# Merge of a hybrid attention block: three shared staging places for both branches' outputs, and w_out loaded block by block

## The chip, the cores and the metric

One core of a Trainium2 chip runs the whole kernel. The metric is the device time of one execution in microseconds (us), as the median of several. Five engines work side by side, each on its own list of instructions in a fixed order: PE multiplies matrices, DVE (vector), ACT (scalar) and POOL (GpSimd) work on tiles, and SP (sync) issues most of the DMA transfers. An instruction that waits holds back everything behind it on its own engine.

## The reference, cut to what matters

```
proj = rms_norm(x) @ w_in              # split into q, k, v, gates of two branches
o_diff = differential attention (4 heads), normalised, times silu(gate)   # (1024, 512)
o_mla  = latent attention (4 heads), times silu(gate)                     # (1024, 512)
merged = sigmoid(g_diff) * (o_diff @ w_proj_diff) + sigmoid(g_mla) * (o_mla @ w_proj_mla)
x = x + merged @ w_out                 # w_out is 1024 x 1024
return rms_norm(x, norm_final)
```

All is float32. Each factor of a product is split into a high part (`...h`, a cast on ACT) and a low part (`...l`, the rest, a subtraction on DVE or POOL), and a product of tiles is three PE instructions: high by high, low by high, high by low (`mm3`, L160 to L162). The product with w_out is a scheme of seven products of half-size blocks, for which sums and differences of blocks of w_out are made first.

## The kernel before, in words

The differential branch runs first; its outputs are written to DRAM (`d_od`, four heads of 128 x 1024). The latent branch follows and writes its outputs to `d_om`. Gates are kept in DRAM as `d_t`. The merge begins while the last latent head is still in work:

- `merge_begin` makes the pools and loads the differential outputs: 8 half tiles of 128x512 (256 KB each) from `d_od` into the tile `or`, of which there is one, and splits each into `odh` (ACT) and `odl` (DVE). A load into a tile starts only when the last reader of the earlier content is done.
- Then `product(0, j)` multiplies them by w_proj_diff, for eight column blocks j in the order `JO`, in two halves of 12 PE instructions each. For each half a gate tile `tg` (three places) is loaded, and DVE multiplies it with the product in PSUM: the eviction, L1023, into `part` or `mr`. There are two PSUM banks `mm` for all this, so a half can start when the eviction of an earlier one has freed a bank. The weights come by `load_p` through `wpr`, are cast to `wph` on ACT and get `wpl` from POOL.
- The first two blocks j of `product(0, ...)` are mixed with the last values step of the latent branch (`mla_values`: transposes L457, split into `ph` and `pl`, products into `pv`). `take` loads the latent outputs from `d_om` through `omr` (two places) in the meantime and splits them into `omh`, `oml`.
- The remaining six blocks, `JO[2:]`, follow. Meanwhile w_out (4 MB) comes in three bursts: `load_b1` (four loads of 256 KB), `load_b2` (four of 512 KB), `load_b12` (four of 256 KB), and `weight_sums(i)` splits the blocks and makes their sums on DVE and POOL (L1128, L1138).
- Then `product(1, j)` for all eight j (latent outputs, no change), and the products with w_out.

When each piece of work is put into the program is set by `defer(ns, fn)`: it is called when a count of nominal PE time has moved on by ns. The order on each engine is settled when the program is built.

Of the kernel before, what the change touches and what calls it, by code (L numbers as in the profile page):

```python
# [14 lines left out]
F32 = mybir.dt.float32  # L15
# [8 lines left out]
P = 128  # L24
# [27 lines left out]
def emit(tc, a):  # L52
    nc = tc.nc
    V, A, G, T = nc.vector, nc.scalar, nc.gpsimd, nc.tensor

    def pool(name, side=None, space=None, bufs=1):
        kw = {}
        if side:
            kw["side"] = side
        if space is not None:  # L60
            kw["space"] = space
        return tc.alloc_tile_pool(name=name, bufs=bufs, reuse_waits="tile", **kw) if space is not DRAM \
            else tc.alloc_tile_pool(name=name, bufs=bufs, **kw)
# [3 lines left out]
    def nm(s):  # L67
        counter[0] += 1
        return f"{s}_{counter[0]}"

    def mk(p, shape, dt, tag, bufs=None):
        return p.tile(shape, dt, name=nm(tag), tag=tag, bufs=bufs)

    def one(p, shape, dt, name):
        return p.tile(shape, dt, name=name, tag=name, bufs=1)
# [14 lines left out]
    def defer(ns, fn):  # L90
        counter[0] += 1
        heapq.heappush(later, (clock[0] + ns, counter[0], fn))
# [18 lines left out]
    def drain():  # L111
        while queue or hook:
            fill(1.0)
# [5 lines left out]
    def drive(gen):  # L119
        for gap in gen:  # L120
            fill(gap)
# [29 lines left out]
    def split(hi, lo, src, eng=None):  # L151
        A.copy(hi, src)  # L152
        (eng or V).tensor_tensor(lo, src, f32(hi), op=ALU.subtract)  # L153
# [10 lines left out]
    def half(n):  # L164
        return slice(n * 512, n * 512 + 512)
# [191 lines left out]
    for si, (base, width, nw) in enumerate(sweeps):  # L357
# [28 lines left out]
        for b in range(NB):  # L386
            raw = mk((p0b, p0c)[si], [P, 384], F32, "raw", 8)
# [452 lines left out]
    def latent_tiles(h):  # L840
        pl = (latent["even"], pl2)[h % 2]
        kns[h] = [mk(pl, [P, S], F32R, "kn" + x, 1) for x in "hl"]
        qns[h] = [mk(pl, [P, S], F32R, "qn" + x, 1) for x in "hl"]
# [8 lines left out]
    def prep(h):  # L852
        w = latent_w.pop(h)
        if h % 2 == 0:
            st = [mk(pl2, [P, S], F32R, f"mqs{m}", 1) for m in range(2)]
            qrs[h], qrs[h + 1] = st
            yield from up(w[2], [0, 1, 2],
                          lambda b, n: qr_use(h, b, n, st))
        if h:
            yield from up_q(h, w)  # L860
        if h < 3:
            latent_w[h + 1] = load_latent_w(h + 1)
# [51 lines left out]
    def mla_group_scores(h, g):  # L914
        pend = None
        for i in range(4 * g, 4 * g + 4):
            cost, normalise = mla_scores(h, i)
            if pend:
                pend()
            pend = normalise  # L920
            yield cost
        pend()
        yield 0

    def mla_values(h, g, gap):
        u = mk(wk, [P, 512], F32, "u", 2)
        nc.sync.dma_start(u, d_mg[h][:, half(g)])
        probs = [mprobs.pop((h, i)) for i in range(4 * g, 4 * g + 4)]
        ov = yield from values(g, probs, lambda kb: mvf[g][:, blk(h)] if kb == 4 * g + 3 else
                                 (mvh[kb][:, blk(h)], mvl[kb][:, blk(h)]), tp_any, gap)  # L930
        o = mk(wk, [P, 512], F32, "g", 2)
        V.tensor_tensor(o, ov, u, op=ALU.mult)
        if (h, g) != (3, 1):
            nc.sync.dma_start(d_om[h][:, half(g)], o)
        else:
            split(p3["o"][1][0][3][:, half(1)], p3["o"][1][1][3][:, half(1)], o)
# [30 lines left out]
    def merge_begin():  # L967
        pb = p3["b"] = pool("p3b", "right")
        p3["o"] = [[], []], [[], []]
        p3["o"][1][0].extend(one(pb, [P, S], F32R, f"omh{k}") for k in range(4))  # L970
        p3["o"][1][1].extend(one(pb, [P, S], F32R, f"oml{k}") for k in range(4))
        for tag, shape, dt, bufs in (("wpr", [P, 4, P], F32, 2), ("wph", [P, 4, P], F32R, 2),
                                     ("wpl", [P, 4, P], F32R, 2), ("tg", [P, 512], F32, 3),
                                     ("omr", [P, 512], F32, 2), ("part", [P, 512], F32, 4)):
            for _ in range(bufs):
                mk(pb, shape, dt, tag, bufs)
        pa = p3["a"] = pool("p3a", "right")
        for k in range(4):
            h_ = one(pa, [P, S], F32R, f"odh{k}")
            l_ = one(pa, [P, S], F32R, f"odl{k}")  # L980
            for n in range(2):
                r = mk(pa, [P, 512], F32, "or", 1)
                nc.sync.dma_start(r, d_od[k][:, half(n)])
                split(h_[:, half(n)], l_[:, half(n)], r)
            p3["o"][0][0].append(h_)
            p3["o"][0][1].append(l_)
        p3["w"] = deque()
        p3["plan"] = deque((br, j) for br in range(2) for j in JO)
        for _ in range(2):
            load_p()  # L990

    def load_p():
        if p3["plan"]:
            br, j = p3["plan"].popleft()
            pa = p3["b"]
            wr = mk(pa, [P, 4, P], F32, "wpr", 2)
            nc.sync.dma_start(wr, a[("w_pd", "w_pm")[br]][j])
            wh = mk(pa, [P, 4, P], F32R, "wph", 2)
            wl = mk(pa, [P, 4, P], F32R, "wpl", 2)
            split(wh, wl, wr, G)  # L1000
            p3["w"].append((wh, wl))
# [32 lines left out]
    def group_and_next(h):  # L1034

        other = up_k(h + 1, latent_w[h + 1])
        for i, cost in enumerate(mla_group_scores(h, 1)):
            yield cost
            if i < 2:
                for _ in range(2):  # L1040
                    yield next(other)

    for h in range(4):
        if h < 3:
            latent_tiles(h + 1)
            queue.append(group_and_next(h))
        else:
            queue.append(mla_group_scores(h, 1))
        drive(mla_values(h, 0, 1300))
        drain()  # L1050
        if h < 3:
            queue.append(prep(h + 1))
            drain()
            if h == 2:
                p2v.release()
                latent["even"].release()
                latent["w"].release()
                latent["pool"].release()
                merge_begin()
            queue.append(mla_group_scores(h + 1, 0))  # L1060
        else:
            pl2.release()
            pb = p3["b"]
            queue.append(product(0, JO[0], done_d))
            queue.append(product(0, JO[1], done_d))

            def take(k, n):
                r = mk(pb, [P, 512], F32, "omr", 2)
                nc.sync.dma_start(r, d_om[k][:, half(n)])
                defer(3500, lambda: split(p3["o"][1][0][k][:, half(n)], p3["o"][1][1][k][:, half(n)], r))  # L1070

            for n in range(2):
                for k in range(4 - n):
                    defer(1500 * (4 * n + k), lambda k=k, n=n: take(k, n))
            fill(4000)
        drive(mla_values(h, 1, 700))
        drain()
# [17 lines left out]
    b11 = [one(p3w, [P, 512], F32, f"b11_{i}") for i in range(4)]  # L1095
    b12 = [one(p3w, [P, 512], F32, f"b12_{i}") for i in range(4)]
    b2 = [one(p3w, [P, D], F32, f"b2_{i}") for i in range(4)]

    def load_b1():
        for i in range(4):  # L1100
            nc.sync.dma_start(b11[i], a["w_out"][i][:, half(0)])

    def load_b2():
        for i in range(4):
            nc.sync.dma_start(b2[i], a["w_out"][4 + i])

    def load_b12():
        for i in range(4):
            nc.sync.dma_start(b12[i], a["w_out"][i][:, half(1)])

    def left_operand(n, i, src):
        t = left_set[n, i] = mk(p3["s"], [P, 2, 512], F32R, f"a{n % 2}{i}", 1)
# [2 lines left out]
    def right_operand(n, i, src, eng=None):  # L1115
        t = right_set[n, i] = mk(p3["d"] if n % 3 == 2 else p3w, [P, 2, 512], F32R, f"b{n % 3}{i}", 1)
        split(t[:, 0], t[:, 1], src, eng)
# [12 lines left out]
    def weight_sums(i):  # L1130

        b21, b22 = b2[i][:, half(0)], b2[i][:, half(1)]
        right_operand(0, i, b11[i])
        right_operand(1, i, b21)
        sub(G, b11[i], b12[i], b11[i])
        sub(V, b12[i], b22, b12[i])
        sub(V, b21, b21, b22)
        G.tensor_tensor(b21, b21, b11[i], op=ALU.add)  # L1138

    defer(1000, load_b1)  # L1140
    defer(6000, load_b2)
    defer(11000, load_b12)
    for i in range(4):
        defer(18000 + 5000 * i, lambda i=i: weight_sums(i))
    for j in JO[2:]:
        queue.append(product(0, j, done_d))
    drain()
# [198 lines left out]
```

## Time and profile before

| | |
|---|---|
| median of 3 runs | 909.52 us (907.31 to 910.62) |
| the profiled execution | 907.61 us, of which its trace spans 905.9 us |
| PE busy | 870.4 us (96%) |
| DVE, ACT, POOL busy | 580.5, 349.1, 286.9 us |
| mean granted clock of PE | 0.984 of full speed |

Times in the rows further down count from the start of the span. The merge's differential products lie between 700.8 and 774.2 us of it.

### The profile page before, as it was taken

The page shows a single profiled execution, that of the slowest core. Times are in us where ns is not written, and L with a number is a line of the kernel's source. Part 1 is how long each engine was busy: PE and PEld are TensorE (multiplying, and loading weights), DVE is VectorE, ACT ScalarE, POOL GpSimd, SP SyncE. Part 2 cuts the span into 40 slices and gives each one's busy share as a digit, 9 for nine tenths or more (in the row PEclk, how much of TensorE's full clock was granted, in tenths as well). Part 3 has the DMA queues.
Part 4 walks back from the last instruction along what each step waited for, and adds up shares of the span by engine and source line. Part 5 has one row for each costly group of instructions (what it writes and reads, how often), then busy time and mean ns, then how long its engine had stood idle before and what let it go on. Part 6 is the DMA issues. An engine that isn't in the chain of part 4 may idle for free.

```text
span 905.9 us, 11737 instructions
## 1 busy us (share of the span) xinstructions
PE 870.4 (96%) x4308; PEld 709.7 (78%) x4308; DVE 580.5 (64%) x1064; ACT 349.1 (39%) x690; POOL 286.9 (32%) x207
## 2 busy tenths in 40 slices
PE   9989999999999999999999999999999788999995
PEld 6879988787887878878777877688787476888884
DVE  5573257738287573874768485866867474689765
ACT  6652162334224242133423344545546340113442
POOL 2432013222241131422213222732313026485651
PEclk9999999999999999999999999999999797999998
DMA  8874035121222322312211216301025373435004
GB/s 291 292 204 137 22 128 175 59 82 70 82 71 69 93 71 71 93 50 90 94 33 58 76 56 221 99 13 47 24 62 183 127 264 107 140 117 209 1 24 164
DMA packets 49979, 96.74 MB, mean 107 GB/s; under 512 B 5120, under 2 KB 17664, under 8 KB 49920
## 3 DMA queue, kind: packets, MB, share of 16 engines
q1 hardware_dynamic: 47328, 89.81, 30.2%
q0 software_dynamic: 1152, 3.67, 1.3%
q10 hardware_dynamic: 1440, 2.49, 0.7%
q8 instruction: 34, 0.56, 0.3%
q14 instruction: 25, 0.20, 0.1%
HBM read 68.96 MB, written 27.00 MB: 106 GB/s over the span
## 4 chain that ended last, share of the span: by engine, by line
PE 80%; DVE 7%; DMA 6%; ACT 2%; issue 2%; POOL 2%; SPq 0%; POOLq 0%; DVEq 0%; ACTq 0%
PE mm L160 18%; PE mm L162 17%; PE mm L161 17%; PE sc L619 4%; PE acc L160 2%; PE acc L162 2%; PE acc L161 2%; PE tp L457 2%; PE bank L161 2%; PE bank L160 2%; PE bank L162 2%; PE pv L161 2%; PE pv L160 2%; PE pv L162 2%; DMA big<-in_xT 1%
## 5 line engine op out<-in xcount | busy, mean ns | idle before, releaser
L160 PE MATMUL mm<-hh,wh 128*128 128x512 f32 x512 | 205.9, 402 | 0.0
L162 PE MATMUL mm<-hh,wl 128*128 128x512 f32 x512 | 200.2, 391 | 0.0
L161 PE MATMUL mm<-hl,wh 128*128 128x512 f32 x512 | 199.9, 390 | 0.0
L153 POOL TENSOR_TENSOR wl<-wr,wh 128x1024 fp32r<-128x1024 f32 x32 | 81.8, 2557 | 240.2 <-ACT wh L152 240.2
L160 PEld LDWEIGHTS mm<-hh,wh 128*128 128x128 f32 x512 | 96.2, 188 | 25.0 <-issue 3.8
L162 PEld LDWEIGHTS mm<-hh,wl 128*128 128x128 f32 x512 | 96.1, 188 | 21.1
L161 PEld LDWEIGHTS mm<-hl,wh 128*128 128x128 f32 x512 | 96.3, 188 | 18.0
L438 ACT ACTIVATE e<-sc,mn 128x128 f32<-128x128 f32 (+3 forms) x64 | 47.5, 743 | 82.9 <-DVE mn L435 80.0
L435 DVE CUSTOM_DVE_ANT_0 sc<-sc,mask 128x128 f32<-128x128 f32 (+7 forms) x96 | 71.6, 772 | 8.7 <-PE sc L902 7.2
L153 DVE TENSOR_TENSOR pl<-tp,ph 128x512 fp32r<-128x512 f32 (+2 forms) x52 | 31.5, 606 | 63.9 <-ACT ph L152 63.8
L152 ACT CAST ph<-tp 128x512 fp32r<-128x512 f32 (+2 forms) x52 | 27.1, 520 | 87.5 <-PE tp L457 85.9
L152 ACT CAST wh<-wr 128x1024 fp32r<-128x1024 f32 x32 | 33.5, 1049 | 38.5 <-PE mm L161 28.6
L911 POOL TENSOR_TENSOR e<-e,rs 128x128 f32<-128x128 f32 (+5 forms) x24 | 25.4, 1063 | 66.0 <-DVE rs L443 65.2
L160 PE MATMUL bank<-wch,hh 128*128 128x384 f32 (+1 forms) x128 | 42.3, 332 | 3.3 <-ACT wch L152 3.3
L161 PE MATMUL acc<-b,a 128*128 128x512 f32 (+1 forms) x116 | 44.5, 383 | 0.0
L160 PE MATMUL acc<-b,a 128*128 128x512 f32 (+1 forms) x116 | 44.4, 383 | 0.0
L162 PE MATMUL acc<-b,a 128*128 128x512 f32 (+1 forms) x116 | 44.4, 383 | 0.0
L569 DVE TENSOR_TENSOR g<-mm,rbc 128x512 f32<-128x512 f32 x40 | 27.5, 687 | 25.5 <-PE mm L162 25.0
L161 PE MATMUL bank<-wcl,hh 128*128 128x384 f32 (+1 forms) x128 | 42.3, 330 | 0.6 <-DVE wcl L153 0.6
L153 POOL TENSOR_TENSOR wpl<-wpr,wph 128x512 fp32r<-128x512 f32 x16 | 21.2, 1323 | 67.6 <-ACT wph L152 62.7
L162 PE MATMUL bank<-wch,hl 128*128 128x384 f32 (+1 forms) x128 | 41.9, 328 | 0.0
L160 PE MATMUL mm<-odh,wph 128*128 128x512 f32 x64 | 28.0, 443 | 10.4 <-DVE mr L1023 5.9
(310 smaller groups left out, 1984.5 us busy)
## 6 DMA issues: line engine op xcount, KB each, us to landing
wr<-in_w_t SPq DMA_DIRECT2D x32, 512.0 KB, 3.6
d_t<-u SPq DMA_DIRECT2D x32, 256.0 KB, 2.0
tg<-d_t SPq DMA_DIRECT2D x32, 256.0 KB, 2.8
big<-in_x SPq DMA_DIRECT2D x8, 512.0 KB, 7.6
xres<-in_x SPq DMA_DIRECT2D x8, 512.0 KB, 7.9
big<-in_xT SPq DMA_DIRECT2D x7, 512.0 KB, 6.6
craw<-d_c SPq DMA_DIRECT2D x5, 512.0 KB, 6.1
d_mg<-u SPq DMA_DIRECT2D x8, 256.0 KB, 3.6
```

The source lines that it names most:

```text
L152: A.copy(hi, src)
L153: (eng or V).tensor_tensor(lo, src, f32(hi), op=ALU.subtract)
L160: T.matmul(ps, lhsT=lh, rhs=rh, start=first, stop=False, skip_group_check=skip)
L161: T.matmul(ps, lhsT=lh, rhs=rl, start=False, stop=False, skip_group_check=skip)
L162: T.matmul(ps, lhsT=ll, rhs=rh, start=False, stop=last, skip_group_check=skip)
L435: V.tensor_tensor_reduce(sc[:, 0:W], sc[:, 0:W], mask[:, S - W:S], scale=-scale, scalar=BIG, op0=ALU.add, op1=ALU.min, accum_out=mn)
L438: A.activation(dst, sc[:, 0:W], AF.Exp, scale=-1.0, bias=mn, accum_out=sm)
L457: T.transpose(tp[:, blk(j)], probs[j][:, blk(kb)], ident)
L569: V.tensor_tensor(g, b, rbc[:, half(n)], op=ALU.mult)
L619: T.matmul(sc[m][:, c0:c0 + n], lhsT=q[r, blk(i)], rhs=k[r, c0:c0 + n], start=x == 0, stop=x == 2)
L911: G.tensor_tensor(e, e, r.broadcast_to([P, W]), op=ALU.mult)
```

## The change

The tile `or` goes. A tile `raw` with three places takes both the differential outputs (in `merge_begin`) and, later, the latent ones (in `take`, which had `omr` with two places). The three bursts of w_out are replaced by `load_b(i)`, one for each of the four blocks of rows: it loads the block's first half row, then, after steps of nominal time, its lower block and its second half row, and puts `weight_sums(i)` behind them. The blocks start 7000 nominal ns apart. Nothing is computed differently, and the number of loads and of instructions is the same.

```
--- before.py
+++ after.py
-                                     ("omr", [P, 512], F32, 2), ("part", [P, 512], F32, 4)):
+                                     ("raw", [P, 512], F32, 3), ("part", [P, 512], F32, 4)):
...
             for n in range(2):
-                r = mk(pa, [P, 512], F32, "or", 1)
+                r = mk(pb, [P, 512], F32, "raw", 3)
                 nc.sync.dma_start(r, d_od[k][:, half(n)])
                 split(h_[:, half(n)], l_[:, half(n)], r)
...
             def take(k, n):
-                r = mk(pb, [P, 512], F32, "omr", 2)
+                r = mk(pb, [P, 512], F32, "raw", 3)
                 nc.sync.dma_start(r, d_om[k][:, half(n)])
...
-    def load_b1():
-        for i in range(4):
-            nc.sync.dma_start(b11[i], a["w_out"][i][:, half(0)])
-
-    def load_b2():
-        for i in range(4):
-            nc.sync.dma_start(b2[i], a["w_out"][4 + i])
-
-    def load_b12():
-        for i in range(4):
-            nc.sync.dma_start(b12[i], a["w_out"][i][:, half(1)])
+    def load_b(i):
+        nc.sync.dma_start(b11[i], a["w_out"][i][:, half(0)])
+        defer(2300, lambda: nc.sync.dma_start(b2[i], a["w_out"][4 + i]))
+        defer(4600, lambda: nc.sync.dma_start(b12[i], a["w_out"][i][:, half(1)]))
+        defer(10000, lambda: weight_sums(i))
...
-    defer(1000, load_b1)
-    defer(6000, load_b2)
-    defer(11000, load_b12)
     for i in range(4):
-        defer(18000 + 5000 * i, lambda i=i: weight_sums(i))
+        defer(2000 + 7000 * i, lambda i=i: load_b(i))
```

What this does to the order on the engines is seen in three places. The first is SP, at the begin of the merge. Before, loads of `d_od` (into `or`) stand one by one among those of the weights, gates and latent outputs:

```order
L983 DMA or_6491<-d_od 128x512
L997 DMA wpr_6529<-in_w_pd 128x512
L997 DMA wpr_6535<-in_w_pd 128x512
L1010 DMA tg_6808<-d_t_82 128x512
L1069 DMA omr_6814<-d_om 128x512
L1069 DMA omr_6822<-d_om 128x512
L983 DMA or_6495<-d_od 128x512
L1010 DMA tg_6829<-d_t_82 128x512
L997 DMA wpr_6861<-in_w_pd 128x512
L1010 DMA tg_6871<-d_t_82 128x512
```

In the change the same place of SP's list reads:

```order
L983 DMA raw_6492<-d_od 128x512
L983 DMA raw_6496<-d_od 128x512
L983 DMA raw_6502<-d_od 128x512
L997 DMA wpr_6530<-in_w_pd 128x512
L997 DMA wpr_6536<-in_w_pd 128x512
L1010 DMA tg_6809<-d_t_82 128x512
L983 DMA raw_6506<-d_od 128x512
L983 DMA raw_6512<-d_od 128x512
L983 DMA raw_6516<-d_od 128x512
L1010 DMA tg_6830<-d_t_82 128x512
```

All eight loads of `d_od` now stand ahead of the first load of `d_om`, three in a row.

The second place is ACT, in the last values step of the latent branch (`e` is a row block of probabilities, `ph` the high part of its transpose, `omh` the high part of latent outputs from `raw`). In the change it reads:

```order
L438 ACTIVATE e7_1517_6782,sm_1520_6796<-sc_1518_6783,mn_1519_6794 128x1024
L152 CAST ph_1546_6855<-mm_1543_6848 128x512
L152 CAST wph_1549_6864<-wpr_1548_6862 128x512
L152 CAST ph_1558_6886<-tp_1557_6881 128x512
L152 CAST omh3_6466<-raw_1544_6853 128x512
L152 CAST omh0_6463<-raw_1554_6878 128x512
L152 CAST omh1_6464<-raw_1560_6898 128x512
L152 CAST ph_1563_6910<-mm_1562_6905 128x512
```

Casts of `odh` no longer stand here; three casts of latent outputs stand ahead of the third `ph`.

The third is DVE, in the six remaining blocks of `product(0, ...)` (`mr...` is an eviction; `b2_0` is the lower block 0 of w_out, `b11_0` and `b12_0` the half rows of the upper one; `b00`, `b10` and so on are low parts of split blocks). Before, sums of all four blocks stand together:

```order
L1023 SCALAR_TENSOR_TENSOR mr5_7018<-tg_1603_7102,mm_1604_7104 128x512
L1023 SCALAR_TENSOR_TENSOR mr2_7015<-tg_1608_7124,mm_1609_7126 128x512
L1128 TENSOR_TENSOR b2_3_7039<-b2_3_7039 128x512
L1128 TENSOR_TENSOR b12_0_7032<-b2_0_7036,b12_0_7032 128x512
L1128 TENSOR_TENSOR b12_1_7033<-b2_1_7037,b12_1_7033 128x512
L1128 TENSOR_TENSOR b12_2_7034<-b2_2_7038,b12_2_7034 128x512
L1128 TENSOR_TENSOR b12_3_7035<-b2_3_7039,b12_3_7035 128x512
L1023 SCALAR_TENSOR_TENSOR mr2_7015<-tg_1610_7144,mm_1611_7146 128x512
```

In the change each block's sums stand between evictions (the evictions shown are those of the 3rd to the 6th of twelve halves):

```order
L1023 SCALAR_TENSOR_TENSOR mr5_7019<-tg_1602_7081,mm_1603_7083 128x512
L1122 TENSOR_TENSOR b12_0_7033<-b2_0_7037,b12_0_7033 128x512
L153 TENSOR_TENSOR b01_1628_7201<-b11_1_7030,b01_1628_7201 128x512
L1023 SCALAR_TENSOR_TENSOR mr5_7019<-tg_1604_7098,mm_1605_7100 128x512
L153 TENSOR_TENSOR b11_1629_7204<-b2_1_7038,b11_1629_7204 128x512
L1122 TENSOR_TENSOR b2_1_7038<-b2_1_7038 128x512
L1122 TENSOR_TENSOR b12_1_7034<-b2_1_7038,b12_1_7034 128x512
L1023 SCALAR_TENSOR_TENSOR mr2_7016<-tg_1612_7121,mm_1613_7123 128x512
L153 TENSOR_TENSOR b02_1645_7268<-b11_2_7031,b02_1645_7268 128x512
L1023 SCALAR_TENSOR_TENSOR mr2_7016<-tg_1616_7148,mm_1617_7150 128x512
```

At most one difference `b12_i` (L1122, L1128 before) stands ahead of any eviction: `b12_0` ahead of that of the 4th half, with `b01` between, `b12_1` ahead of the 5th, `b12_2` ahead of the 8th, with `b03` between, and `b12_3` ahead of the 10th, with a difference of `b2_3` between. On SP the loads of w_out are spread in the same way, one or two of a block and then a gate tile or a weight: the load of `b12_0` stands right behind the other two of its block, those of `b12_1`, `b12_2` and `b12_3` behind the gate tiles of the 6th, 8th and 10th half.

## Rows read from the trace of the kernel before

**Rows 1.** The page, busy us of each engine, share of the span, instructions.
```profile
PE 870.4 (96%) x4308; PEld 709.7 (78%) x4308; DVE 580.5 (64%) x1064; ACT 349.1 (39%) x690; POOL 286.9 (32%) x207
```

**Rows 2.** Stretches: length, busy us by engine, PE's clock, DMA share, GB/s.
```profile
677.20:700.80 23.60, 22.27 (x132) 18.98 (x131) 17.86 (x41) 15.73 (x36) 7.46 (x8) 1.00 0.59 197
700.80:730.30 29.50, 22.98 (x96) 16.23 (x95) 15.30 (x24) 10.96 (x20) 4.22 (x3) 0.83 0.33 108
730.30:774.20 43.90, 38.04 (x151) 30.43 (x150) 23.95 (x29) 8.47 (x15) 18.87 (x13) 0.88 0.60 202
774.20:818.50 44.30, 44.30 (x197) 36.54 (x196) 33.91 (x40) 9.12 (x15) 27.93 (x19) 1.00 0.37 114
...
710.00:720.00 10.00, 7.05 (x18) 4.57 (x19) 6.46 (x10) 4.70 (x9) 0.19 (x1) 0.54 0.39 129
```

**Rows 3.** Waits between 670 and 780: total us, times, longest.
```profile
PE mm L160 <- DVE mr L1023: 5.9, 2, 3.1
...
ACT odh L152 <- DMA or<-d_od: 4.8, 4, 2.8
...
PE mm L160 <- ACT odh L152: 4.6, 2, 3.1
```

**Rows 4.** The chain that ended last, 700 to 720: start, us, what.
```profile
703.02 3.12 DMA or<-d_od
...
706.16 0.63 ACT odh L152
...
706.81 0.70 DVE odl L153
...
707.53 3.21 DMA or<-d_od
```

**Rows 5.** SP's timeline, the first and the last of eight loads of d_od.
```profile
675.72 0.40 SPq L983 DMA_DIRECT2D or<-d_od  x1
...
712.13 0.32 SPq L983 DMA_DIRECT2D or<-d_od  x1
```

**Rows 6.** PE's timeline: the first product of the merge, and two later marks.
```profile
700.77 0.48 PE L160 MATMUL mm<-odh,wph 128*128 128x512 f32 x1
...
719.24 0.39 PE L161 MATMUL pv<-pl,mvh 128*128 128x512 f32 x1
...
730.26 0.39 PE L160 MATMUL mm<-odh,wph 128*128 128x512 f32 x1
```

**Rows 7.** The chain that ended last, 730 to 762.
```profile
737.12 8.77 DMA tg<-d_t
...
749.84 1.72 POOL b L1128
...
756.40 1.75 DVE b L1128
```

**Rows 8.** Groups on DVE, then POOL, 730.3 to 774.2: busy us, mean ns.
```profile
L1023 DVE SCALAR_TENSOR_TENSOR mr<-tg,mm 128x512 f32<-128x512 f32 x11 | 7.3, 682 | 12.7 <-PE mm L162 12.7
L153 DVE TENSOR_TENSOR b<-b,b 128x512 fp32r<-128x512 f32 x8 | 6.3, 815 | 0.1
L1128 DVE TENSOR_TENSOR b<-b,b 128x512 f32<-128x512 f32 x4 | 5.9, 1491 | 3.6 <-POOL b L1128 3.6
L1128 DVE TENSOR_TENSOR b<-b 128x512 f32<-128x512 f32 x4 | 3.7, 937 | 0.1
...
L153 POOL TENSOR_TENSOR wpl<-wpr,wph 128x512 fp32r<-128x512 f32 x5 | 6.5, 1294 | 19.5 <-ACT wph L152 14.5 <-DMA tg<-d_t 5.0
L1128 POOL TENSOR_TENSOR b<-b,b 128x512 f32<-128x512 f32 x4 | 5.7, 1425 | 2.2 <-DVE b L1128 2.2
```

**Rows 9.** DMA issues between 670 and 800: KB each, median us to landing.
```profile
tg<-d_t SPq DMA_DIRECT2D x27, 256.0 KB, 2.9
...
b<-in_w_out SPq DMA_DIRECT2D x8, 256.0 KB, 6.3
b<-in_w_out SPq DMA_DIRECT2D x4, 512.0 KB, 9.4
```

## The prediction, made before the changed kernel ran

> **What bounds the kernel now.** I read the page first: PE is busy 96% of the span [rows 1], so only time in which PE stands still, or runs at a lower clock, can be won. The stretches say where that is [rows 2]. From 774.2 to 818.5, with latent products alone, PE is busy all of 44.3 us at full clock: 192 products of the merge and 3 behind them, 0.227 us each. That is my price for one PE instruction on 512 columns. From 700.8 to 730.3, with the first differential products and the last values step, it is busy 23.0 of 29.5 us at a mean clock of 0.83. From 730.3 to 774.2, with the other six blocks, it is 38.0 of 43.9 us at 0.88. I call these stages A and B. The clock belongs to the loss: between 710 and 720, where PE has just stood still, it was granted 0.54 of full speed [rows 2].
>
> The waits name the releasers [rows 3]. In A, PE waits 4.6 us for `odh` from ACT, and ACT 4.8 us for the loads of `or`. In B, PE waits 5.9 us in two waits for the eviction `mr` on DVE.
>
> The chain shows A's mechanism: load 3.1 us, cast 0.63, low part 0.70, next load 3.2, and so on [rows 4]. There is one place, so each load starts only after the split before it. The eight loads run from 675.72 to 712.13 [rows 5]: seven steps in 36.4 us, 5.2 us each, while PE wanted the first head at 700.77 and all four soon after.
>
> In B the chain goes through a gate tile that was under way for 8.77 us [rows 7], against a median of 2.9 [rows 9]. It was issued behind bursts of w_out, whose loads took 6.3 us (256 KB) and 9.4 us (512 KB) [rows 9]. Then it goes through sums on POOL and a difference on DVE of 1.72 and 1.75 us [rows 7], behind which an eviction stood.
>
> **Stage A, the sum.** What PE did from 700.77 to 719.24 [rows 6] is, by its order, 28 products and 8 transposes. The products cost 28 x 0.227 = 6.4 us. A transpose has no row of its own at full rate; it lies between nothing and a full product, and I take half, 0.11 us, as it has a quarter of the columns but a load of its own: 0.9 us. So 7.3 us of work (6.4 to 8.2) took 18.5 us, and 11.2 us can be won (10.3 to 12.1).
>
> With three places the loads go in three rounds. At 5.2 us a round the last is in at about 677 + 3 x 5.2 = 693, and even at 7.5 us it is in by 700, when PE wants it. So the waits for `odh` go. The loads now compete with the weights `wpr` at 677 to 682, and the casts of `odh` stand between the attention's casts on ACT. PE has score products that it can do there, and 23.6 us of stretch in which it loses only 1.3 [rows 2]. I take nothing for it; the third rival prices it.
>
> What is late next is the latent outputs. On ACT three casts `omh` stand ahead of the third `ph`, and the first needs the output of head 3, which must be evicted, written to `d_om` and read back. The scores end at 700.8 [rows 6]. Three vector steps of 0.7 (as the evictions of [rows 8]), a write and a read of 3.1 each (the nearest row is a load of this size, [rows 4]), and three casts of 0.63 [rows 4] give 711.0. PE wants that `ph` after its 7.3 us and another 14 products and 4 transposes (3.6 us), at 711.7. That just fits. A transfer 1 us late costs 0.3 us, 4 us late 3.3 us. I take 0.7 us, bounds 0 and 3. A gains **10.5 us** (7.3 to 12.1).
>
> **Stage B, the sum.** Its 144 products are 32.7 us, and 0.4 us is left over from the values step. 43.9 less 33.1 leaves 10.8 us to win. A half is 12 x 0.227 = 2.73 us, and its bank is wanted again two halves later, so an eviction may be one half late.
>
> The burst goes: at most one block's 1 MB and one gate tile are now under way. The question is a wait that the change adds. DVE does the difference `b12_i`, which waits for POOL's sum over the same tile, which waits for the load of `b12_i`. Behind it on DVE stands an eviction, and behind that PE. Let L be the time that this load takes, and count from B's start.
>
> - Block 1: its load stands on SP behind the gate tile of the 6th half, which waits for the 3rd eviction: 3 x 2.73 + 0.7 + two issues, 9.2. Then L, POOL 1.43, the difference 1.49, the 5th eviction 0.68 [rows 8]. PE wants its bank at the 7th half, at 16.4. Slack: L may be 3.6.
> - Block 2: behind the gate tile of the 8th half, which waits for the 5th eviction (16.5), so issued at 16.9. Then L + 1.43 + 1.49, a low part of 0.82, and the 8th eviction, 0.68 [rows 8]. Wanted at the 10th half, 24.6. L may be 3.3.
> - Block 3: behind the gate tile of the 10th half, issued at 20.5. Then L + 1.43 + 1.49 + 0.94 + 0.68, wanted at the 12th half, 30.0. L may be 5.0.
> - Block 0: issued at 1.5, wanted through the 4th eviction at 13.7. Then L + 1.43 + 1.49 + 0.82 + 0.68. L may be 7.8.
>
> The nearest row for L, 256 KB without a burst, is the gate tile's 2.9 us; in a burst it was 6.3 [rows 9]. At 2.9 nothing is lost. At 6.3 the blocks lose 2.7, 3.0, 1.3 and 0, together 7.0 us. I take 2.9, as the load has at most some 0.75 MB ahead of it, where the burst's had up to 4 MB, and 1.0 us for what is late in some block. B gains **9.8 us** (3.8 to 10.8).
>
> A rule that speaks against this: differences on DVE with two inputs in SBUF took 1.49 us on the mean, and one 1.75 us while POOL was at work, against 0.68 for an eviction that reads PSUM [rows 7, 8]. The Trainium skill (SBUF — State Buffer, section "SBUF: two separate sides") says that such a DVE operation and a POOL operation that reads SBUF lock a shared port pair against each other, and the loser blocks for the whole instruction. The rows agree, and I have priced the differences at the blocked mean. By the rule all sixteen low parts and differences in B could be blocked; at 1.75 us they would be 28 us, with twelve evictions 36 us, so DVE rather than PE would set B, and B would gain 7 us in place of 9.8.
>
> **The sum.** 907.61 for the profiled execution (span 905.9 and 1.7 around it) less 10.5 less 9.8 gives 887.3. The median of the runs lies 1.9 above the profiled execution; I add about 1 and say **888 us**.
>
> **The rivals.**
>
> 1. *A gains, B only partly (0.11).* The loads of w_out still take 6.3 us each: 907.6 - 10.5 - 10.8 + 7.0 = 893.3. DVE as the bound gives about 890. For it: twelve gate tiles, weights and 4 MB still share the stage, 202 GB/s before [rows 2]. Against it: no burst is queued.
> 2. *B gains, A only partly (0.07).* The attention's casts on ACT stand behind eight casts that wait for loads in three rounds. Before, ACT waited in four such places, 1.2 us on the mean [rows 3]; five arrivals of the second and third round at that price are 6 us on the path to the last scores: 887.3 + 6 = 893. For it: ACT works in order. Against it: the loads come well before they are wanted only if nothing else is slow there, and PE has scores to do.
> 3. *No change (0.04).* Not the loads but the last head's softmax and DVE set both stages, and PE waits for them instead. The time stays about 907. Against it: the chain of A holds only loads and splits of `d_od` for 9 us [rows 4].
> 4. *Slower (0.04).* One mechanism: DVE's wait at the four differences. With the slacks above, the loss over the blocks at L is (L - 3.6) + (L - 3.3) + (L - 5.0) + (L - 7.8). It eats all of 21.3 at about L = 10.3, and at L = 12 it is 28.3: 907.6 - 21.3 + 28.3 = 914.6. For it: 512 KB took 9.4 us in the burst [rows 9], and a gate tile 8.77 [rows 7]. Against it: those stood in the burst that goes.
>
> **How the numbers follow.** That both stages gain nearly all has 0.74, with its own range 884.5 to 891. Rivals 1 and 2 reach to 898 if their prices double in part. From 884.5 to 898 the first three cases are held, more than 8 in 10 with room for one that I have not seen. What a measurement can tell from no change is about 0.5%, 4.5 us; faster by more than that has 0.91 (0.74 + 0.11 + 0.07, less a little), within it 0.05, slower 0.04.
>
> **What would show it.** Right: PE's first differential product near 700.8 as before, no wait of PE for `odh`, the mark that stood at 730.26 [rows 6] near 719 to 720, B of 33 to 35 us, full clock in both, and the eight loads of `d_od` issued by about 690. Wrong in A: ACT waiting for `raw` while PE waits for `ph` or `e`. Wrong in B: PE waiting for `mr` while DVE waits for POOL, and loads of w_out that land after 6 us or more. The stage from 774.2 on should be as long as before.

## The result, and the profile after

The changed kernel took 893.26 us (median; 892.58 to 896.05) beside 908.55 us for the kernel before on the same chip. The ratio is 0.9835, with a 95% interval of 0.9806 to 0.9865, so it is faster by 1.65%, some 15 us. Forecast were 888 us and a range of 884.5 to 898. The direction and the two places were right; the gain came out a quarter smaller than forecast (15.3 us, where the sum had 20.3). The profiled execution took 893.56 us with a span of 891.9.

The stretches of the changed kernel that answer to [rows 2], with the same columns: ahead of the merge's first product, A, B, and the latent products.

```profile
678.76:703.41 24.65, 23.15 (x132) 18.80 (x131) 21.14 (x45) 17.59 (x40) 7.30 (x7) 1.00 0.70 221
703.41:723.70 20.29, 19.32 (x96) 14.87 (x95) 13.27 (x22) 8.50 (x16) 4.92 (x4) 1.00 0.37 119
723.70:760.35 36.65, 34.40 (x150) 27.22 (x149) 23.96 (x30) 8.41 (x14) 19.46 (x13) 1.00 0.70 228
760.35:804.20 43.85, 43.85 (x194) 36.15 (x193) 33.38 (x39) 9.14 (x15) 27.95 (x19) 1.00 0.41 127
```

PE's clock is at full speed in all four, where A had 0.83 and B 0.88. A is 20.29 us long, between the marks at 700.77 and 730.26 [rows 6] it was 29.49; B is 36.65 us, where it was 43.92 to the first latent product at 774.18. Both parts of the loss shrank: in A PE stands still for 1.0 us (20.29 less 19.32 busy), where it was 6.5 [rows 2], in B for 2.3, where it was 5.9; the rest of the gain, 3.7 and 3.6 us, is less busy time for the same products, at the higher clock.

PE's waits between 660 and 800 (total us, times, longest), which answer to [rows 3]:

```profile
PE mm L160 <- DVE mr L1023: 2.2, 3, 0.8
...
PE pv L160 <- ACT ph L152: 0.6, 2, 0.3
PE mm L457 <- DVE part L1023: 0.4, 1, 0.4
PE mm L160 <- DVE pl L153: 0.3, 1, 0.3
```

The wait for `odh` (4.6 us before) is gone; that for `mr` went from 5.9 to 2.2. SP's timeline shows why the first is gone: the eight loads of `d_od` start in three rounds and are all issued by 691.6, where the last one started at 712.13 [rows 5].

```profile
678.27 1.47 SPq L983 DMA_DIRECT2D raw<-d_od  x3
...
683.39 3.71 SPq L983 DMA_DIRECT2D raw<-d_od  x3
...
690.71 0.92 SPq L983 DMA_DIRECT2D raw<-d_od  x2
```

The landings between 670 and 790, which answer to [rows 9]: w_out's loads are faster than in the bursts (6.3 and 9.4 us), but slower than a gate tile.

```profile
tg<-d_t SPq DMA_DIRECT2D x28, 256.0 KB, 3.1
...
b<-in_w_out SPq DMA_DIRECT2D x8, 256.0 KB, 4.2
b<-in_w_out SPq DMA_DIRECT2D x4, 512.0 KB, 4.8
```

What B still loses stands in DVE's timeline (start, length, line, operation, idle time before it and who ended it):

```profile
730.46 2.36 DVE L153 TENSOR_TENSOR b<-b,b 128x512 fp32r<-128x512 f32 x2
732.85 1.67 DVE L1122 TENSOR_TENSOR b<-b 128x512 f32<-128x512 f32 x1
734.44 0.68 DVE L1023 SCALAR_TENSOR_TENSOR mr<-tg,mm 128x512 f32<-128x512 f32 x1
735.04 1.46 DVE L1122 TENSOR_TENSOR b<-b,b 128x512 f32<-128x512 f32 x1
736.42 1.78 DVE L153 TENSOR_TENSOR b<-b,b 128x512 fp32r<-128x512 f32 x1
738.13 0.68 DVE L1023 SCALAR_TENSOR_TENSOR mr<-tg,mm 128x512 f32<-128x512 f32 x1
738.72 0.68 DVE L153 TENSOR_TENSOR b<-b,b 128x512 fp32r<-128x512 f32 x1
739.44 0.69 DVE L1122 TENSOR_TENSOR b<-b 128x512 f32<-128x512 f32 x1
741.32 0.69 DVE L1122 TENSOR_TENSOR b<-b,b 128x512 f32<-128x512 f32 x1 [1.19 <-POOL b L1122]
741.93 0.68 DVE L1023 SCALAR_TENSOR_TENSOR mr<-tg,mm 128x512 f32<-128x512 f32 x1
```

Two things hold the evictions back. From 730.46 to 738.13 DVE never waits, but five operations that take 0.69 us elsewhere take 7.3 us together; PE then waits 0.58 us for the eviction that starts at 738.13. At 741.32 a difference has waited 1.19 us for POOL, and the eviction behind it costs PE 0.84 us. POOL had waited 2.23 us for the load of `b12`. PE's third wait, 0.82 us, stands behind the 8th eviction, ahead of which a difference waited 1.22 us for POOL and a low part took 1.50 us.

**Comparing single executions.** The program ahead of the merge is not changed, but its last product (`mm<-ch,wqnl`) starts at 676.90 in the profiled execution before and at 678.76 in that after; over the fourteen profiled executions of this study it lies between 674.98 and 680.10. So below I count from that product. The lead-in runs from it to the first `mm<-odh`, A from there to the third block's first product, B to the first `mm<-omh`, the rest to the span's end; all are starts of rows in PE's timeline. A ratio is to the runs of the kernel before that were taken beside it, whose medians lie between 907.2 and 908.6 us.

| kernel | lead-in | A | B | from the product to the end | median us | ratio to before |
|---|---|---|---|---|---|---|
| before | 23.87 | 29.49 | 43.92 | 229.00 | | |
| changed | 24.65 | 20.29 | 36.65 | 213.14 | 893.26 | 0.9835 |
| places alone | 24.13 | 20.69 | 43.37 | 219.63 | 897.91 | 0.9886 |
| spread alone | 23.59 | 30.87 | 36.58 | 222.51 | 900.72 | 0.9918 |
| sums later | 23.64 | 20.16 | 37.04 | 212.32 | 892.29 | 0.9823 |
| latent loads later | 24.20 | 20.08 | 37.51 | 213.27 | 893.27 | 0.9830 |
| two places | 23.66 | 19.89 | 37.35 | 212.37 | 892.28 | 0.9831 |
| two places, four gates | 23.88 | 19.93 | 35.30 | 210.60 | 891.17 | 0.9801 |
| no sums | 23.76 | 20.78 | 33.79 | 210.43 | 890.50 | 0.9801 |
| sums on DVE | 23.56 | 21.05 | 34.94 | 211.73 | 892.77 | 0.9820 |
| one place | 24.29 | 29.01 | 38.85 | 223.64 | 903.76 | 0.9965 |
| bursts, no sums | 23.56 | 20.56 | 34.36 | 210.38 | 890.86 | 0.9815 |
| four gates, sums on DVE | 24.38 | 19.40 | 34.56 | 209.82 | 888.17 | 0.9790 |
| four gates, first difference on DVE | 24.41 | 19.85 | 34.69 | 210.73 | 890.00 | 0.9803 |

The ratios have intervals of 0.15 to 0.3% to either side, so they part the halves of the change, but not steps of 1 or 2 us. Those are read from the columns A and B.

### The profile page after: what moved, and what is told of

It reads as the page before. It is cut to its first block, busy times and chain, and to the rows that moved or that the text cites. A ratio compares the mean times of both kernels' runs of the same rounds, so it can differ in the third digit from the quotient of the medians.

```text
span 891.9 us, 11736 instructions
## 1 busy us (share of the span) xinstructions
PE 865.0 (97%) x4308; PEld 705.6 (79%) x4308; DVE 580.2 (65%) x1064; ACT 349.1 (39%) x690; POOL 287.8 (32%) x207
## 4 chain that ended last, share of the span: by engine, by line
PE 79%; DVE 7%; DMA 5%; issue 3%; ACT 2%; POOL 2%; SPq 1%; POOLq 0%; DVEq 0%; ACTq 0%
PE mm L160 17%; PE mm L162 16%; PE mm L161 16%; PE sc L619 4%; PE acc L160 2%; PE acc L162 2%; PE acc L161 2%; PE tp L457 2%; PE bank L161 2%; PE bank L160 2%; PE bank L162 2%; PE pv L161 2%; PE pv L162 1%; PE pv L160 1%; DMA b<-in_w_out 1%
## 5 line engine op out<-in xcount | busy, mean ns | idle before, releaser
L153 DVE TENSOR_TENSOR b<-b,b 128x512 fp32r<-128x512 f32 x24 | 29.7, 1265 | 5.7 <-ACT b L152 5.5
```

## Experiments

**1. The places alone, and the spread alone.** Each half of the change by itself; the first keeps the three bursts of w_out and the sums in their old places, the second the single `or` and the two `omr`. The edits are shown against the changed kernel, cut to what matters.

```
-    def load_b(i):
...
+    defer(1000, load_b1)
+    defer(6000, load_b2)
+    defer(11000, load_b12)
...
+        defer(18000 + 5000 * i, lambda i=i: weight_sums(i))
```

> First half of the change by itself: the eight d_od loads and the seven d_om loads go through the three shared places, the w_out blocks come in the three bursts of before. Theory (the two halves add up): the stretch from the first differential product to the product after the last values step is about 20.3 us long as in the changed kernel (29.5 before), the first product some 0.8 us late as there, and the merge's stretch with the bursts is 43.9 us as before; so 8.4 us less than before, about 900 us, ratio about 0.991. Rival (the halves lean on each other: with the first products early, the bursts meet other transfers or the delayed casts): the burst stretch becomes longer than 45 us and the kernel gains less than 6 us (over 902.5); or, the other way, it becomes shorter than 42 us and the kernel ends below 898.

```
-                r = mk(pb, [P, 512], F32, "raw", 3)
+                r = mk(pa, [P, 512], F32, "or", 1)
                 nc.sync.dma_start(r, d_od[k][:, half(n)])
...
-                r = mk(pb, [P, 512], F32, "raw", 3)
+                r = mk(pb, [P, 512], F32, "omr", 2)
```

> Second half by itself: w_out comes one block at a time, the differential outputs load through the single place and the main outputs through their two, as before. Theory (the halves add up): the first stretch stays near 29.5 us with its waits for odh, the merge's stretch falls from 43.9 to about 36.6 us as in the changed kernel; 7.3 us less than before, about 901.3 us, ratio about 0.992. Rival (the spread loads collide with something that the first stretch's lateness leaves behind): the merge's stretch over 39 us, the kernel over 903.5.

The halves add up. From the unchanged product on, the places alone give 229.00 - 219.63 = 9.4 us, the spread alone 6.5, together 15.9, which is what the changed kernel gives (229.00 - 213.14). By medians they are 1.1% and 0.8%. Each half moves its own stage: A is 20.69 with places and 30.87 without, B 36.58 with the spread and 43.37 without. The places alone ended 2 us below their theory's 900 and just below the rival's 898, but B did not fall under the rival's 42; the spread alone ended within 1 us of its theory's 901.3. That A of the spread alone is 1.4 us longer than in the kernel before is seen in one execution and not explained. The two stretches of the spread alone, A first; its clock (the third number from the right) is still down in A, in B it is full:

```profile
699.98:730.85 30.87, 24.06 (x97) 17.15 (x95) 15.17 (x24) 10.96 (x20) 4.22 (x3) 0.78 0.31 104
730.85:767.43 36.58, 34.63 (x151) 27.12 (x149) 24.49 (x30) 8.40 (x14) 19.19 (x13) 1.00 0.71 228
```

The kernel with the places alone is also the cleanest view of what the bursts and their sums do to B, since A no longer runs into it. DVE's timeline there:

```profile
741.30 1.27 DVE L1023 SCALAR_TENSOR_TENSOR mr<-tg,mm 128x512 f32<-128x512 f32 x2
742.50 1.80 DVE L1128 TENSOR_TENSOR b<-b 128x512 f32<-128x512 f32 x1
744.22 6.83 DVE L1128 TENSOR_TENSOR b<-b,b 128x512 f32<-128x512 f32 x4
750.97 1.27 DVE L1023 SCALAR_TENSOR_TENSOR mr<-tg,mm 128x512 f32<-128x512 f32 x2
```

Between two pairs of evictions stand five differences of 1.7 us each in a heap, 8.5 us without a break, and PE has two banks. POOL's row of sums has no break from 740.91 to 752.18 either, so neither engine waits for a load of w_out in this heap. Such an operation takes 0.69 us elsewhere; five of them would then be 3.5 us (an estimate), so more than half of the heap's 8.5 us goes with POOL's sums, which run beside it all the time. Behind the eviction PE's products take 0.43 us, not 0.23, until about 755.5: the granted clock is 0.50 from 752.5 to 755.0, the lower of its two levels. This stall was paid for twice.

```profile
752.91 0.43 PE mm L160
...
756.08 0.24 PE mm L162
```

**2. Putting off the sums, or the latent loads.**

```
-        defer(10000, lambda: weight_sums(i))
+        defer(13500, lambda: weight_sums(i))
```

> The changed kernel with each block's casts and differences put off by 3.5 us of TensorE work (10000 to 13500), loads untouched, so that each block's loads have about 9 us of TensorE work, not 5.4, between the last issue and the first use. Theory (what stage B still loses is the differences' wait for their loads, passed from POOL to DVE and from there to PE): DVE's waits for POOL's difference fall from 3.6 us to under 1, PE's waits for mr (2.2 us) vanish, the merge's stretch goes from 36.65 to 34 us or less, and the kernel is 2 to 3 us faster than the changed one, about 890.5. Rival (the loss is DVE's and POOL's work itself, slowed when both run: 1.5 to 1.8 us in place of 0.69): the waits move but the stretch stays above 36 us, the kernel within 1 us of the changed one (892.5 to 894).

```
-                    defer(1500 * (4 * n + k), lambda k=k, n=n: take(k, n))
+                    defer(9000 + 1500 * (4 * n + k), lambda k=k, n=n: take(k, n))
```

> The changed kernel with the seven d_om loads and their casts put off by 9 us of TensorE work, past the last values step. Theory (the first stretch's two remaining losses, DVE late by 1.2 us at the last softmax because of the oml low parts, and 0.34 to 0.7 us at the third transposed tile behind the omh casts, come from the place of the d_om work): first product 0.5 to 0.8 us earlier, the first stretch about 0.5 us shorter, the kernel about 1 us faster than the changed one, about 892. Rival (the d_om loads then compete with w_out's in the merge): the merge's stretch longer than 37.5 us, and the kernel slower than the changed one, 893.5 to 895.

Neither tells the theories apart, as the rows on every engine came out in the same order as in the changed kernel; only the tiles' numbers differ. Calling a piece later by nominal time did not move it. That makes them two repeats of the changed kernel, which is how I use them: B is 36.65, 37.04 and 37.51 in the three (mean 37.1), A 20.29, 20.16 and 20.08 (mean 20.2), the lead-in 24.65, 23.64 and 24.20. Differences under about 1 us in B or in the lead-in are thus no verdict.

**3. How many places.**

```
-                                     ("raw", [P, 512], F32, 3), ("part", [P, 512], F32, 4)):
+                                     ("raw", [P, 512], F32, 2), ("part", [P, 512], F32, 4)):
...
```

> The changed kernel with two shared places in place of three. Theory (stage A's stall was the single place, and any number that has all eight loads in by about 700 will do): four rounds of two loads at 5.1 to 7.3 us a round (the starts of the changed kernel's rounds lie 5.1 and 7.3 us apart) end at about 700, just when PE wants the first head; no wait of PE for odh over 0.5 us, stage A (first differential product to the third block's first product) about 20.5 us, the kernel within 1.5 us of the changed one, about 893. Rival (the third place matters: the last round and the latent loads behind it come late): waits for odh or for the third transposed tile of 1.5 to 4 us, stage A of 22 to 24.5 us, the kernel 895 to 897.5.

> The changed kernel with a single shared place for both the differential and the latent outputs. Theory (what cost stage A was the number of places alone: one load at a time, 5.2 us each): the eight d_od loads again run until about 714, PE waits 4 to 5 us for odh, stage A 29.5 to 31 us, stage B about 37 us, the kernel about 901 as with the spread alone. Rival (sharing one place puts seven more loads in the same row and the latent ones reach the second half of the merge late): the kernel above 905.

Two places do as well as three: A 19.89, B as in the repeats. The rounds are short enough that the last head is in before PE wants it. With one, A is 29.01 and PE waits 3.9 us for `odh`, much as before. SP's timeline with one place, the first loads, and the latent ones behind them:

```profile
679.55 0.32 SPq L983 DMA_DIRECT2D raw<-d_od  x1
...
710.28 4.34 SPq L983 DMA_DIRECT2D raw<-d_od  x2
...
739.45 0.33 SPq L1069 DMA_DIRECT2D raw<-d_om  x1
```

The theory's 901 us was missed by 3: the seven latent loads follow in the same row, the last of them issued at 751.57, and B is 38.85, 1.8 us longer than in the repeats, with waits of PE for `mr` of 3.9 us. So the rival had the right place, but the kernel stayed below its 905. Where the rest of the 3 us lies is not shown.

**4. What the sums cost in B, and what the burst costs.** Two kernels leave out the three differences and the addition of each block, with the loads spread and in bursts.

```
-        sub(G, b11[i], b12[i], b11[i])
-        sub(V, b12[i], b22, b12[i])
-        sub(V, b21, b21, b22)
-        G.tensor_tensor(b21, b21, b11[i], op=ALU.add)
```

> The changed kernel with the three differences and the addition of each w_out block left out (the splits and all loads stay), so that its last products take the loaded blocks as they are. It measures what the sums cost in stage B by any mechanism. Theory: all of stage B's loss against its 33.1 us of PE work comes from the sums, stage B 33.1 to 33.8 us, the kernel about 3 us faster than the changed one, about 890. Rival (the loss comes from gate tiles and weights that land late among 4 MB, with or without sums): stage B above 35 us, the kernel at 892 or more.

> The kernel of the first half alone (three places, w_out in three bursts) with the three differences and the addition of each block left out, splits and loads kept; its last products take the blocks as they are. With bursts and sums stage B was 43.4 us, with spread loads and no sums 33.8. Theory (the burst itself cost the time: a gate tile under way for 8.8 us behind it holds the eviction): stage B stays above 40 us. Rival (the bursts matter only through the sums, which come late and in a heap on DVE and POOL): stage B falls to 34 to 36 us.

Spread and without sums, B is 33.79 us, near the 33.1 of PE's work: the changed kernel and its repeats lose 2.9 to 3.7 us to the sums, and 0.7 us to anything else. In bursts without sums it is 34.36. So here the theory fell: the burst by itself costs 0.6 us, less than the repeats differ (PE waits once for `mr`, 0.9 us), where bursts and sums together cost 43.37 - 33.79 = 9.6. Yet its loads are nearly as slow as in the kernel before (6.3 and 9.4 us [rows 9]), and the gate tile issued at 728.03 was under way for 9.26 us; the kernel's landings between 715 and 762, that gate tile in its chain, and its stretch B:

```profile
tg<-d_t SPq DMA_DIRECT2D x14, 256.0 KB, 2.7
b<-in_w_out SPq DMA_DIRECT2D x8, 256.0 KB, 6.2
b<-in_w_out SPq DMA_DIRECT2D x4, 512.0 KB, 8.2
```
```profile
728.03 9.26 DMA tg<-d_t
```
```profile
723.54:757.90 34.36, 33.43 (x150) 27.43 (x149) 15.38 (x22) 8.29 (x14) 6.46 (x5) 1.00 0.75 257
```

So what the spread won came from taking the heap of operations on DVE and POOL apart, not from faster transfers. This is read from the two kernels without sums and from the heap shown above; no run keeps the bursts and spreads the sums alone, or keeps the heap and leaves POOL without sums.

**5. What the rest of B's loss is.** Two edits. Four gate tiles (with two `raw`, for the memory) let SP issue what stands behind a gate tile up to half a block sooner.

```
-            t = mk(p3["b"], [P, 512], F32, "tg", 3)
+            t = mk(p3["b"], [P, 512], F32, "tg", 4)
...
```

> Two shared places, and the memory of the third given to the gate tiles, which then have four. Theory (stage B loses what the prediction's formula says: the difference waits for POOL, POOL for the load of b12, and the load stands on SP behind a gate tile that waits for an eviction): with four gate tiles each such load is issued up to one half, 2.7 us, sooner, so the slacks of 3.6, 3.3 and 5.0 us become 6.3, 6.0 and 7.7, the loads of 4.0 to 6.2 us fit, PE's waits for mr (2.2 us in the changed kernel) go below 0.7 and stage B from 36.6 to about 34.5 us: about 2 us less than with two places and three gates. Rival (DVE's and POOL's own work, slowed when both run, sets the evictions late): stage B stays above 36 us and the PE's waits for mr near 2 us.

All sums on DVE leave POOL with the weights' low parts alone; with that DVE no longer waits for a result of POOL either, so this edit bears on both suspects.

```
-        sub(G, b11[i], b12[i], b11[i])
+        sub(V, b11[i], b12[i], b11[i])
...
-        G.tensor_tensor(b21, b21, b11[i], op=ALU.add)
+        V.tensor_tensor(b21, b21, b11[i], op=ALU.add)
```

> The changed kernel with all three differences and the addition of each w_out block on DVE, so that POOL has only the weights' low parts there. Theory (DVE's operations on two SBUF tiles are slowed by POOL's running at the same time: 1.1 to 1.8 us in place of 0.69): DVE's low parts and differences take 0.7 us apart from a few beside wpl, its busy time in stage B is about the same in spite of eight more operations, PE's waits for mr fall below 1 us, stage B is 34 to 35.5 us, the kernel 1 to 2 us faster than the changed one, about 891.5. Rival (the loads of b12 are the cause): DVE then waits for the loads itself, 3 us or more in all, and stage B stays at 36.5 us or more.

Both helped in B, by 37.1 - 35.30 = 1.8 and 37.1 - 34.94 = 2.2 us. With four gates DVE's wait for POOL's difference falls from 3.6 to 1.4 us, PE's for `mr` to 0.9, and DVE's operations stay slow. The groups on DVE in B, first of the changed kernel, then with four gates, then with all sums on DVE (busy us, mean ns, then idle time before and who ended it):

```profile
L153 DVE TENSOR_TENSOR b<-b,b 128x512 fp32r<-128x512 f32 x8 | 8.8, 1114 | 2.6 <-ACT b L152 2.6
...
L1122 DVE TENSOR_TENSOR b<-b 128x512 f32<-128x512 f32 x4 | 3.7, 934 | 0.1
L1122 DVE TENSOR_TENSOR b<-b,b 128x512 f32<-128x512 f32 x4 | 3.5, 884 | 3.6 <-POOL b L1122 3.6
```
```profile
L153 DVE TENSOR_TENSOR b<-b,b 128x512 fp32r<-128x512 f32 x8 | 9.5, 1192 | 2.1 <-ACT b L152 2.1
...
L1122 DVE TENSOR_TENSOR b<-b,b 128x512 f32<-128x512 f32 x4 | 3.5, 882 | 1.4 <-POOL b L1122 1.4
```
```profile
L153 DVE TENSOR_TENSOR b<-b,b 128x512 fp32r<-128x512 f32 x8 | 7.0, 882 | 2.8 <-ACT b L152 2.8
L1122 DVE TENSOR_TENSOR b<-b,b 128x512 f32<-128x512 f32 x8 | 6.6, 822 | 0.4 <-DMA b<-in_w_out 0.4
L1122 DVE TENSOR_TENSOR b<-b 128x512 f32<-128x512 f32 x4 | 2.7, 687 | 0.1
L1132 DVE TENSOR_TENSOR b<-b,b 128x512 f32<-128x512 f32 x4 | 2.7, 682 | 0.0
```

With all sums on DVE, eight more operations cost only 2.0 us of its busy time (25.9, against 24.0), as the others came back towards 0.69; and its wait for the loads is 0.4 us, not the 3 us that the rival asked for. PE still waited 1.2 us for `mr`. Most of that kernel's gain in B was given back: A is 0.9 us longer than in the repeats, the part behind B 0.6. So its median, 892.77, shows no difference from the changed one.

**6. Both together, and a smaller edit.**

> Two places, four gate tiles, and all differences and the addition on DVE. The two together if their causes are separate (waits passed on from the loads; operations slowed beside POOL): stage B from 37.0 (mean of four profiled runs of the order of the changed kernel) by 1.7 and 2.1 to about 33.5 us, PE's waits for mr below 0.5, the kernel 1 us faster than with four gates alone, about 890. Rival (both take away the same waits): stage B 34.5 to 35.5 us, the kernel at 891.

The last kernel moves only the first difference, `b12` less `b11`, to DVE.

> Two places, four gate tiles, and only the first difference, b12 less b11, moved from POOL to DVE; the addition stays on POOL. DVE then waits for no result of POOL. Theory: stage B within 0.5 us of the kernel with all sums on DVE. Rival (the additions that stay on POOL slow DVE's operations as before): DVE's operations again 0.9 to 1.2 us on the mean, stage B near 35.3 us as with four gates alone.

B is 34.56 with both, so the two edits take away largely the same waits, as the rival said. With the first difference alone it is 34.69, and no wait of PE for `mr` is left (it waits 1.0 us for weights `wph`). DVE's low parts were 964 ns on the mean there, between the 1192 of four gates and the 882 of all sums on DVE. The four B of 34.56 to 35.30 differ by less than the repeats do, so these runs don't rank the edits. The kernel with both is the fastest of the study: 888.17 us, ratio 0.9790 with an interval of 0.9765 to 0.9814. That interval just overlaps the changed kernel's, so only its lead on the kernel before is certain, 19 us (17 to 21); from the unchanged product on it needs 209.8 us, where the changed one and its repeats need 212.3 to 213.3.

## Why the prediction was right, and where its sizes were off

**Stage A.** Its reading held: one place made the eight loads a chain, more places broke it, and one place in the changed kernel brings the stall back. The rounds were 5.1 and 7.3 us long (forecast 5.2, at most 7.5). The term that was off is the remaining wait: 19.0 us was forecast for A (29.5 - 10.5), and it took 20.2 on the mean of the repeats. The forecast laid 0.7 us on the third `ph` alone. In the changed kernel the piece up to the product that stood at 719.24 [rows 6] took 8.3 us, where the sum had 7.3 and at most 8.2: PE waited 0.40 us for `part` in it, which the sum did not have. The piece behind it took 12.0 us, where 11.0 and the 0.7 were forecast: 0.3 were lost at the third `ph`, since the latent outputs took 3.9 to 4.4 us to read back, not 3.1, and 0.34 in a wait for `pl`. None stands out.

**The lead-in.** "I take nothing for it" was nearly right. It grew by 0.78 us in the first profile, but the three repeats average 24.2 against 23.87 and 23.59 without the places: 0.3 to 0.6 us, less than the repeats differ (23.64 to 24.65), and not the 6 of the second rival. PE had scores to do there, and ACT's waits for `raw` (1.11, 0.44 and 0.89 us) mostly fell beside them.

**Stage B: the step that failed.** The prediction read the chain's gate tile of 8.77 us as the cause, and "the burst goes" as the gain. The kernel with bursts and no sums contradicts that: a gate tile took 9.26 us in it, and B was 34.36. In the kernel before that gate tile landed at 745.89 (737.12 and 8.77 us [rows 7]), but DVE's timeline has it at work on low parts and differences without a break from 740.49 to 746.95, so the eviction at 746.87 would have come hardly earlier.

```profile
743.34 1.68 DVE L1128 TENSOR_TENSOR b<-b 128x512 f32<-128x512 f32 x1
744.94 0.68 DVE L153 TENSOR_TENSOR b<-b,b 128x512 fp32r<-128x512 f32 x1
745.66 0.69 DVE L1128 TENSOR_TENSOR b<-b 128x512 f32<-128x512 f32 x1
746.27 0.68 DVE L153 TENSOR_TENSOR b<-b,b 128x512 fp32r<-128x512 f32 x1
746.87 1.28 DVE L1023 SCALAR_TENSOR_TENSOR mr<-tg,mm 128x512 f32<-128x512 f32 x2
748.06 0.68 DVE L1128 TENSOR_TENSOR b<-b 128x512 f32<-128x512 f32 x1
748.66 1.76 DVE L1128 TENSOR_TENSOR b<-b,b 128x512 f32<-128x512 f32 x1
751.59 0.69 DVE L1128 TENSOR_TENSOR b<-b,b 128x512 f32<-128x512 f32 x1 [1.17 <-POOL b L1128]
754.71 3.44 DVE L1128 TENSOR_TENSOR b<-b,b 128x512 f32<-128x512 f32 x2 [2.43 <-POOL b L1128]
758.07 1.27 DVE L1023 SCALAR_TENSOR_TENSOR mr<-tg,mm 128x512 f32<-128x512 f32 x2
```

PE's second wait, 2.78 us, was for differences alone, DVE's own and POOL's: none of DVE's evictions starts between 748 and 758. DVE was busy 23.95 us in B before [rows 2] and 23.96 after. So its work became no less; as far as the runs show, the 7.3 us that B gained came from its standing apart. That B gained all the same is in part luck: the edit that took the burst away moved the sums too.

**Stage B: the term that was mis-sized.** Forecast were 34.1 us, measured 36.65, in the repeats up to 37.5. For the load's time L the prediction took 2.9 us, the gate tile's; the loads of `b12` took 6.2, 4.2, 4.0 and 4.9 us for blocks 0 to 3. With these its formula gives (4.2 - 3.6) + (4.0 - 3.3) = 1.3 us lost, at blocks 1 and 2; PE waited 0.84 and 0.82 us there. The formula has no loss at block 0, yet PE waited 0.58 us behind its operations: it had them at the means of the kernel before (a low part 0.82, five operations 4.9 us), and the five took 7.3. So PE's waits for `mr` were 2.2 us in all, 2.4 and 3.2 in the repeats. Of its signs for being wrong in B, PE's wait for `mr` while DVE waits for POOL came, loads of 6 us and more did so only once.

The experiments on B show the wait as a cause: four gates shorten it and give back 1.8 us. They don't show the price of the slow operations apart from it. All sums on DVE take away both and give back 2.2, both edits together 2.5; and with four gates and the first difference alone on DVE, where that wait is gone and low parts still take 0.96, it is 2.4. That the slow operations cost PE something is seen in the 0.58 us above.

**The rule on the shared ports.** By it B was to gain 7 us in place of 9.8 (43.9 less the 36 of DVE's work make it 7.9), and it gained 6.4 to 7.3. The size fits by luck, the mechanism only in part. DVE did not set B: it was busy 24.0 of 36.65 us, not 36. But operations of DVE did take up to 1.78 us while POOL worked, and with all sums on DVE their means were 0.68 to 0.88. That agrees with the Trainium skill (SBUF — State Buffer, "SBUF: two separate sides"), by which a DVE operation with two inputs in SBUF and a POOL operation that reads SBUF shut each other out for a whole instruction.

**The sum.** From the unchanged product on, the first profile gained 15.9 us and its repeats 15.7 and 16.7, where 20.3 was forecast: 1.2 short in A, 0.3 in the lead-in, 3.0 in B. The part behind B did not move (131.7 us before, 131.6 after), as forecast. The profiled execution shows 14.0 because its unchanged first part was 1.9 us slower.

## What to carry to other kernels

For a staging place, count rounds: loads divided by places, times one load with its split, against the moment the last one is wanted. Here two places gave all that three did. When a chain passes through a slow transfer and then through a heap of vector work, take the work away in an experiment before blaming the transfer; and look at what stands between two evictions in the vector engine's row, for PE can run ahead of the evictions only by as many halves as it has banks. And compare single executions from the last instruction that the change can't have touched.

## What the hardware showed that I had not expected

- In the changed kernel and its halves a DVE operation of 0.69 us on two SBUF tiles took up to 1.8 us beside POOL's work on SBUF, and POOL's took 1.7 to 1.8 instead of 1.29: now one pays and now the other, low parts and differences alike.
- After PE's waits of 4.1 and 2.4 us in B of the places alone, products took 0.43 us, not 0.23, for 3 us more (granted clock 0.50 from 752.5 to 755.0); with single waits of 0.6 to 0.8 us in the changed kernel, and of up to 1.87 us with one place, B's clock was 1.00.
- The last product ahead of the merge, behind the same instructions, started between 675.0 and 680.1 us in fourteen executions, a spread larger than most effects studied here.
